# Average pooling on one core: runs of 126 KB per partition instead of 64 KB, and the stores moved into the load queue

## The chip, the cores and the metric

The kernel runs on one core of a Trainium2 chip. The metric is device time in microseconds (us) of one execution. The engines that matter are VectorE (DVE in the profile), which does the sums, ScalarE (ACT), which scales and issues some stores, SyncE (SP), which issues the loads, and the core's sixteen DMA engines, which move all data between HBM and the on-chip memory SBUF. A DMA that spans 128 partitions is spread over all sixteen DMA engines, eight partitions on each.

## The reference

Average pooling in one dimension with window 4 and stride 4 over float32 data of 64 x 256 x 8192:

```python
def reference(x, kernel_size, stride):          # 4 and 4
    out_len = (length - kernel_size) // stride + 1
    for i in range(out_len):
        start = i * stride
        output[:, :, i] = np.mean(x[:, :, start : start + kernel_size], axis=2)
```

The windows do not overlap and rows divide evenly, so the whole input can be taken as one flat run of 134,217,728 numbers, in which every four neighbours give one output. 536.87 MB are read and 134.22 MB written.

## The kernel before

The flat input is cut into 64 blocks. A block is 128 partitions of `RUN = 16384` numbers, 64 KB each and one behind the other in HBM, so it is 8 MB without a gap. Its output is 2 MB: 16 KB for each partition, again without a gap.

`load` issues one DMA of a whole block in SP's queue (line 44). Two input buffers `xt` are in turn. `sums` does two additions on VectorE: line 50 adds neighbours within `xt` and writes the half-size result over the front of the same tile; line 54 adds neighbours of that into an output tile `r`. `scale` (line 59) multiplies `r` by 1/4 in place on ScalarE. An output tile has room for two blocks, and there are two of them.

The order of the work is that of the program, engine by engine. SP issues a load when VectorE has finished line 54 for the block that was in that buffer. For the first `SINGLES = 8` blocks, ScalarE scales and stores each block by itself (line 75, 2 MB). After that it scales two blocks with one instruction and stores them with one DMA of 4 MB (line 78), in which each partition has two runs of 16 KB that lie 2 MB apart in HBM. All these stores are in ScalarE's own queue, so the DMA engines see two queues: SP's with loads and ScalarE's with stores.

At the end the last block is loaded in two pieces (`LAST`, 5 MB and 3 MB) into one buffer, and the last stores are issued by SP: a pair (line 87), a single block (line 90) and two pieces (line 95).

Of the kernel before, what the change touches and what calls it, by code (L numbers as in the profile page):

```python
# [1 line left out]

# [4 lines left out]


RUN = 16384

SINGLES = 8
LAST = (10240, 6144)


@with_exitstack
def kernel(
    ctx: ExitStack,
    tc: tile.TileContext,
    x: bass.AP,
    kernel_size: bass.AP,  # L20
    stride: bass.AP,
    out: bass.AP,
):
    nc = tc.nc
    K, S = int(kernel_size), int(stride)
    assert K == S == 4
    B, C, L = x.shape
    P = nc.NUM_PARTITIONS
    dt = x.dtype
    M = RUN // K  # L30
    blocks = B * C * L // (P * RUN)
    assert blocks * P * RUN == B * C * L and L % K == 0 and blocks % 2 == 0
    assert sum(LAST) == RUN

    xb = x.rearrange("b c l -> (b c l)").rearrange("(n p m) -> n p m", p=P, m=RUN)
    ob = out.rearrange("b c l -> (b c l)").rearrange("(n p m) -> n p m", p=P, m=M)

    pin = ctx.enter_context(tc.tile_pool(name="xin", bufs=2))
    pout = ctx.enter_context(tc.tile_pool(name="res", bufs=2))

    def load(i, a=0, b=RUN, xt=None):
        if xt is None:
            xt = pin.tile([P, RUN], dt, name="xt")
        nc.sync.dma_start(out=xt[:, a:b], in_=xb[i][:, a:b])
        return xt

    def sums(o, xt, a=0, b=RUN):
        v = xt[:, a:b].rearrange("p (m k) -> p m k", k=2)
        h = xt[:, a : (a + b) // 2]
        nc.vector.tensor_tensor(  # L50
            out=h, in0=v[:, :, 0], in1=v[:, :, 1], op=mybir.AluOpType.add
        )
        w = h.rearrange("p (m k) -> p m k", k=2)
        nc.vector.tensor_tensor(  # L54
            out=o, in0=w[:, :, 0], in1=w[:, :, 1], op=mybir.AluOpType.add
        )

    def scale(o):
        nc.scalar.mul(o, o, 1.0 / K)  # L59

    def edges(cuts):
        at = [sum(cuts[:j]) for j in range(len(cuts) + 1)]
        return list(zip(at[:-1], at[1:]))

    def both(i):
        return ob[i : i + 2].rearrange("n p m -> p n m")

    for i in range(0, blocks - 2, 2):
        r = pout.tile([P, 2, M], dt, name="r")
        for h in range(2):  # L70
            xt = load(i + h)
            sums(r[:, h, :], xt)
            if i < SINGLES:
                scale(r[:, h, :])
                nc.scalar.dma_start(out=ob[i + h], in_=r[:, h, :])
        if SINGLES <= i < blocks - 4:
            scale(r[:])
            nc.scalar.dma_start(out=both(i), in_=r[:])

    n = blocks - 1  # L80
    t = pout.tile([P, 2, M], dt, name="r")
    xt = load(n - 1)
    xl = None
    for a, b in edges(LAST):
        xl = load(n, a, b, xl)
    scale(r[:])
    nc.sync.dma_start(out=both(n - 3), in_=r[:])
    sums(t[:, 0, :], xt)
    scale(t[:, 0, :])
    nc.sync.dma_start(out=ob[n - 1], in_=t[:, 0, :])  # L90
    for a, b in edges(LAST):
        o = t[:, 1, a // K : b // K]
        sums(o, xl, a, b)
        scale(o)
        nc.sync.dma_start(out=ob[n][:, a // K : b // K], in_=o)


# [1 line left out]
_INS = ['x', 'kernel_size', 'stride']  # L99
_OUTS = [((64, 256, 2048), 'float32')]  # L100

_NUMBERS = {'kernel_size': 4, 'stride': 4}


# [26 lines left out]
```

## Time and profile before

| what | value |
|---|---|
| median of three runs | 1554.86 us (1554.7 to 1556.03) |
| the profiled execution, its own time | 1554.4 us |
| span of the profile | 1552.6 us |
| VectorE busy | 839.7 us (54%), 130 instructions |
| ScalarE busy | 227.4 us (15%), 39 instructions |
| data moved by DMA | 671.12 MB, mean 432 GB/s |
| a load of 8 MB, from issue to landing | 35.1 us (median) |
| a store of 4 MB by ScalarE, from issue to landing | 52.0 us (median) |
| line 50 on a block; line 54; line 59 on a block | 8.69 us; 4.43 us; 3.62 us |

The span runs from the first to the last event that the profile has of the core; the execution's time is 1.8 us longer. A DMA engine works off packets, each a contiguous piece of memory, and the profile counts them by queue: q1 is SP's, q10 is ScalarE's. "From issue to landing" includes the time in which a DMA stands in its queue behind others. An engine's waits are listed with what ended them, and SP's list is that of its DMA queue: a wait there delays the issue of a transfer, which matters only if the DMA engines have nothing else queued.

### The profile page before, as it was taken

Reading aid. Unit: us, or ns where it says so; the run is one execution under the profiler, and the core shown is the slowest. Engines: PE = TensorE matmul, PEld = TensorE weight load, DVE = VectorE, ACT = ScalarE, POOL = GpSimd, SP = SyncE. Lnnn points to the kernel's source line nnn. Section 1 sums busy time; section 2 is a strip of 40 time slices with the busy share of each in tenths; the row PEclk is TensorE's granted clock in tenths of the full one; section 3 lists DMA queues with packets and bytes.
Section 4 is the critical chain, followed back from the end, with each engine's and each line's share of the span. In section 5 each row is a group of like instructions: output and inputs, shape, how many; then the busy total and the mean of one; then the engine's idle time right before and its main releaser. Section 6 shows DMA issues by size and latency. Waiting matters only on the chain.

```text
span 1552.6 us, 471 instructions
## 1 busy us (share of the span) xinstructions
DVE 839.7 (54%) x130; ACT 227.4 (15%) x39; POOL 0.2 (0%) x4
## 2 busy tenths in 40 slices
DVE  3646556546465464654646546455464554645646
ACT  1111101110111101111011110111101111011111
POOL 0000000000000000000000000000000000000000
DMA  9999999999999999999999999999999999999999
GB/s 417 420 434 438 439 439 439 412 445 444 413 433 435 443 438 439 432 424 429 439 438 433 437 434 419 439 432 438 439 419 434 434 437 439 441 423 442 422 440 400
DMA packets 18292, 671.12 MB, mean 432 GB/s; under 512 B 1649, under 2 KB 1649, under 8 KB 1777
## 3 DMA queue, kind: packets, MB, share of 16 engines
q1 hardware_dynamic: 10064, 545.26, 81.1%
q10 hardware_dynamic: 8224, 125.83, 18.9%
q14 instruction: 4, 0.02, 0.0%
HBM read 536.87 MB, written 134.22 MB: 432 GB/s over the span
## 4 chain that ended last, share of the span: by engine, by line
DMA 71%; DVE 28%; issue 0%; ACT 0%; DVEq 0%
DMA xt<-in_x_dram 71%; DVE xt L50 18%; DVE r L54 9%; ACT r L59 0%; DVEq L54 0%
## 5 line engine op out<-in xcount | busy, mean ns | idle before, releaser
L50 DVE TENSOR_TENSOR xt<-xt 128x8192 f32<-128x8192 f32 (+1 forms) x65 | 556.5, 8561 | 696.1 <-DMA xt<-in_x_dram 696.1
L59 ACT ACTIVATE r<-r 128x8192 f32<-128x8192 f32 (+3 forms) x38 | 226.2, 5951 | 1313.0 <-DVE r L54 1313.0
L54 DVE TENSOR_TENSOR r<-xt 128x4096 f32<-128x4096 f32 (+1 forms) x65 | 283.4, 4360 | 3.9
L59 ACT ACT_TABLE_LOAD x1 | 1.3, 1283 | 0.7 <-PEq L112 0.7
L112 POOL MEMSET const-bfloat16-1.0<- 128x1 bf16 x1 | 0.1, 101 | 0.0
L112 POOL MEMSET const-uint8-127<- 128x1 uint8 x1 | 0.1, 101 | 0.0
L112 POOL MEMSET const-float32-0.0<- 128x1 f32 x1 | 0.1, 98 | 0.2 <-issue 0.2
L112 POOL MEMSET const-float32-1.0<- 128x1 f32 x1 | 0.1, 98 | 0.0
## 6 DMA issues: line engine op xcount, KB each, us to landing
out_dram<-r ACTq DMA_DIRECT2D x26, 4096.0 KB, 52.0
out_dram<-r ACTq DMA_DIRECT2D x8, 2048.0 KB, 31.7
xt<-in_x_dram SPq DMA_DIRECT2D x1, 5120.0 KB, 23.1
out_dram<-r SPq DMA_DIRECT2D x1, 4096.0 KB, 33.0
xt<-in_x_dram SPq DMA_DIRECT2D x1, 3072.0 KB, 30.0
out_dram<-r SPq DMA_DIRECT2D x1, 2048.0 KB, 16.9
out_dram<-r SPq DMA_DIRECT2D x1, 1280.0 KB, 12.9
xt<-in_x_dram SPq DMA_DIRECT2D x63, 35.1
```

The lines of the kernel that those rows point to most:

```text
L50: nc.vector.tensor_tensor(out=h, in0=v[:, :, 0], in1=v[:, :, 1], op=mybir.AluOpType.add)
L54: nc.vector.tensor_tensor(out=o, in0=w[:, :, 0], in1=w[:, :, 1], op=mybir.AluOpType.add)
L59: nc.scalar.mul(o, o, 1.0 / K)
L112: nc = _bacc.Bacc("TRN2", target_bir_lowering=False, num_devices=1)
```

## The change

- A unit of work is now a group: 128 partitions of 126 KB each, one behind the other in HBM. It is loaded in two halves, `h = 0` and `h = 1`, each 63 KB for every partition (`RUN = 16128`), so that the runs of one load lie 126 KB apart. The group's output is 31.5 KB for each partition, without a gap.
- There are 32 groups, and the rest of the data is one block of 64 KB for each partition (`END = 16384`), which is loaded in the two pieces that the last block had before.
- Every half is scaled by itself, right after its sums.
- The first four groups (`SINGLES = 4`) store each half by itself in ScalarE's queue, 15.75 KB for each partition.
- A later group is stored whole, with one DMA of 31.5 KB for each partition, in SP's queue: it is kept in `held` and issued behind the second load of the next group. The last group's store is issued behind the two loads of the end.

```diff
-RUN = 16384
+RUN = 16128
+END = 16384
 
-SINGLES = 8
+SINGLES = 4
...
-    xb = x.rearrange("b c l -> (b c l)").rearrange("(n p m) -> n p m", p=P, m=RUN)
-    ob = out.rearrange("b c l -> (b c l)").rearrange("(n p m) -> n p m", p=P, m=M)
+    xf = x.rearrange("b c l -> (b c l)")
+    of = out.rearrange("b c l -> (b c l)")
+    xb = xf[:body].rearrange("(n p h m) -> n p h m", p=P, h=2, m=RUN)
+    ob = of[: body // K].rearrange("(n p m) -> n p m", p=P, m=2 * M)
+    xe = xf[body:].rearrange("(p m) -> p m", p=P)
+    oe = of[body // K :].rearrange("(p m) -> p m", p=P)
...
-    for i in range(0, blocks - 2, 2):
-        r = pout.tile([P, 2, M], dt, name="r")
-        for h in range(2):
-            xt = load(i + h)
-            sums(r[:, h, :], xt)
-            if i < SINGLES:
-                scale(r[:, h, :])
-                nc.scalar.dma_start(out=ob[i + h], in_=r[:, h, :])
-        if SINGLES <= i < blocks - 4:
-            scale(r[:])
-            nc.scalar.dma_start(out=both(i), in_=r[:])
+    held = None
+    for g in range(groups):
+        r = pout.tile([P, 2 * M], dt, name="r")
+        for h in range(2):
+            xt = load(xb[g, :, h, :], 0, RUN)
+            if h == 1 and held is not None:
+                nc.sync.dma_start(out=ob[held[0]], in_=held[1])
+            o = r[:, h * M : (h + 1) * M]
+            sums(o, xt, 0, RUN)
+            scale(o)
+            if g < SINGLES:
+                nc.scalar.dma_start(out=ob[g][:, h * M : (h + 1) * M], in_=o)
+        if g >= SINGLES:
+            held = g, r[:]
...
-    scale(r[:])
-    nc.sync.dma_start(out=both(n - 3), in_=r[:])
-    sums(t[:, 0, :], xt)
-    scale(t[:, 0, :])
-    nc.sync.dma_start(out=ob[n - 1], in_=t[:, 0, :])
+    nc.sync.dma_start(out=ob[held[0]], in_=held[1])
+    e = pout.tile([P, 2 * M], dt, name="r")
     for a, b in edges(LAST):
-        o = t[:, 1, a // K : b // K]
+        o = e[:, a // K : b // K]
         sums(o, xl, a, b)
         scale(o)
-        nc.sync.dma_start(out=ob[n][:, a // K : b // K], in_=o)
+        nc.sync.dma_start(out=oe[:, a // K : b // K], in_=o)
```

More of the change, by code (lines that the diff above doesn't have):

```diff
@@ L30, with load, sums @@
     M = RUN // K
-    blocks = B * C * L // (P * RUN)
-    assert blocks * P * RUN == B * C * L and L % K == 0 and blocks % 2 == 0
-    assert sum(LAST) == RUN
-    xb = x.rearrange("b c l -> (b c l)").rearrange("(n p m) -> n p m", p=P, m=RUN)
-    ob = out.rearrange("b c l -> (b c l)").rearrange("(n p m) -> n p m", p=P, m=M)
+    total = B * C * L
+    groups = total // (2 * P * RUN)
+    body = groups * 2 * P * RUN
+    assert L % K == 0 and total - body == P * END
+    assert sum(LAST) == END
+    xf = x.rearrange("b c l -> (b c l)")
[4 more added lines that the diff above has]
+    oe = of[body // K :].rearrange("(p m) -> p m", p=P)
     pin = ctx.enter_context(tc.tile_pool(name="xin", bufs=2))
     pout = ctx.enter_context(tc.tile_pool(name="res", bufs=2))
-    def load(i, a=0, b=RUN, xt=None):
+    def load(src, a, b, xt=None):
         if xt is None:
-            xt = pin.tile([P, RUN], dt, name="xt")
-        nc.sync.dma_start(out=xt[:, a:b], in_=xb[i][:, a:b])
+            xt = pin.tile([P, END], dt, name="xt")
+        nc.sync.dma_start(out=xt[:, a:b], in_=src[:, a:b])
         return xt
-    def sums(o, xt, a=0, b=RUN):
+    def sums(o, xt, a, b):
         v = xt[:, a:b].rearrange("p (m k) -> p m k", k=2)
@@ L63, in edges @@
         return list(zip(at[:-1], at[1:]))
-    def both(i):
-        return ob[i : i + 2].rearrange("n p m -> p n m")
-    for i in range(0, blocks - 2, 2):
-        r = pout.tile([P, 2, M], dt, name="r")
+    held = None
+    for g in range(groups):
+        r = pout.tile([P, 2 * M], dt, name="r")
         for h in range(2):
-            xt = load(i + h)
-            sums(r[:, h, :], xt)
-            if i < SINGLES:
-                scale(r[:, h, :])
-                nc.scalar.dma_start(out=ob[i + h], in_=r[:, h, :])
-        if SINGLES <= i < blocks - 4:
-            scale(r[:])
-            nc.scalar.dma_start(out=both(i), in_=r[:])
-    n = blocks - 1
-    t = pout.tile([P, 2, M], dt, name="r")
-    xt = load(n - 1)
+            xt = load(xb[g, :, h, :], 0, RUN)
[8 more added lines that the diff above has]
+            held = g, r[:]
     xl = None
     for a, b in edges(LAST):
-        xl = load(n, a, b, xl)
-    scale(r[:])
-    nc.sync.dma_start(out=both(n - 3), in_=r[:])
-    sums(t[:, 0, :], xt)
-    scale(t[:, 0, :])
-    nc.sync.dma_start(out=ob[n - 1], in_=t[:, 0, :])
+        xl = load(xe, a, b, xl)
+    nc.sync.dma_start(out=ob[held[0]], in_=held[1])
+    e = pout.tile([P, 2 * M], dt, name="r")
     for a, b in edges(LAST):
-        o = t[:, 1, a // K : b // K]
+        o = e[:, a // K : b // K]
         sums(o, xl, a, b)
         scale(o)
-        nc.sync.dma_start(out=ob[n][:, a // K : b // K], in_=o)
+        nc.sync.dma_start(out=oe[:, a // K : b // K], in_=o)
 _INS = ['x', 'kernel_size', 'stride']
```

## The prediction

> **What bounds the kernel now.** I read the page first: its slices, its DMA queues and its chain. The last two columns of a queue's line are MB moved and the share of sixteen engines' span that its packets took.
>
> ```profile
> span 1552.6 us, 471 instructions
> DMA  9999999999999999999999999999999999999999
> DMA packets 18292, 671.12 MB, mean 432 GB/s; under 512 B 1649, under 2 KB 1649, under 8 KB 1777
> q1 hardware_dynamic: 10064, 545.26, 81.1%
> q10 hardware_dynamic: 8224, 125.83, 18.9%
> ```
>
> The DMA engines are full in every slice, and the two queues together take 100.0% of sixteen engines' span. VectorE is busy 54%, ScalarE 15%. (The chain of waits gives DMA 71% and VectorE 28%, but only because it steps from a load to the sums that freed its buffer; the queue was not empty meanwhile, as the waits below show.) The bytes are fixed (536.87 MB read, 134.22 MB written), so a change can act only through what the engines pay beside bytes: packets, gaps, start and end.
>
> The packet counts can be rebuilt. Queue 1 (SP) has 65 loads of 128 packets, one for each partition's whole run, which is 8320; its stores of the end have 256 + 128 + 128 + 128 = 640; and 69 DMAs leave 16 tiny ones each, 1104. The sum is 10064, as printed. Queue 10 (ScalarE) has 26 pair stores of 256, 8 single stores of 128 and 34 x 16: 8224. So a packet is one contiguous run of one partition: 64 KB in a load, 16 KB in a store.
>
> Then SP's waits (microseconds in total, times, longest):
>
> ```profile
> SPq L44 <- DVE r L54: 817.2, 62, 13.2
> SPq L44 <- DMA xt<-in_x_dram: 660.1, 62, 21.1
> ```
>
> SP issues a load when VectorE has freed its buffer, and a load takes 35.1 us from issue to landing (median of the page), against 19.3 us that one takes alone. So the next load is always queued before its turn, and these waits cost nothing.
>
> Last VectorE's timeline, for its first sum starts when a load has landed:
>
> ```profile
> 22.73 8.69 DVE L50 TENSOR_TENSOR xt<-xt 128x8192 f32<-128x8192 f32 x1 [22.73 <-DMA xt<-in_x_dram]
> 42.06 8.69 DVE L50 TENSOR_TENSOR xt<-xt 128x8192 f32<-128x8192 f32 x1 [6.18 <-DMA xt<-in_x_dram]
> ...
> 90.66 8.69 DVE L50 TENSOR_TENSOR xt<-xt 128x8192 f32<-128x8192 f32 x1 [11.07 <-DMA xt<-in_x_dram]
> ...
> 235.78 8.69 DVE L50 TENSOR_TENSOR xt<-xt 128x8192 f32<-128x8192 f32 x1 [10.97 <-DMA xt<-in_x_dram]
> 255.10 8.70 DVE L50 TENSOR_TENSOR xt<-xt 128x8192 f32<-128x8192 f32 x1 [6.17 <-DMA xt<-in_x_dram]
> ...
> 448.65 8.69 DVE L50 TENSOR_TENSOR xt<-xt 128x8192 f32<-128x8192 f32 x1 [11.07 <-DMA xt<-in_x_dram]
> ...
> 1513.12 8.69 DVE L50 TENSOR_TENSOR xt<-xt 128x8192 f32<-128x8192 f32 x1 [11.21 <-DMA xt<-in_x_dram]
> ```
>
> They give three prices. A load with no store beside it takes 42.06 - 22.73 = 19.33 and 255.10 - 235.78 = 19.32 us. A load and a single 2 MB store take (235.78 - 90.66) / 6 = 24.187, so the store costs 4.862. Two loads and a 4 MB pair store take (1513.12 - 448.65) / 22 = 48.385, so that store costs 9.735.
>
> **Rate and packet price.** Twice the single store (9.724) is the pair store (9.735), though it is two DMAs and not one: the price goes by packets and bytes, not by DMAs. A load (8.389 MB) and a single store (2.097 MB) both have 8 packets on each engine, so their difference is bytes alone: 6.291 MB in 14.463 us, 435.0 GB/s. What is left of the single store, 4.862 - 2.097/0.4350 = 0.041 us, is 8 packets at 5.1 ns. The same 0.041 fits the load.
>
> **The change, part by part.** *Runs of 63 KB and stores of 31.5 KB.* Data packets on each engine before: 520 of loads and 64 + 432 + 24 = 520 of stores, 1040 in all. After: loads 64 x 8 + 16 = 528, stores 8 x 8 + 28 x 8 + 16 = 304, together 832. That is 208 fewer; at 5.1 ns, 1.06 us saved. DMAs go from 103 to 104, which by the step above is nothing. Packets of 63 and 31.5 KB lie between sizes that are in the trace.
>
> *The pitch.* A group is now 126 KB for each partition, so neighbouring partitions are no longer 64 KB apart. No row has this pitch. It cannot gain more than all that the packets cost beside bytes, 1040 x 5.1 ns = 5.3 us. For a loss the nearest bound is the slowest block of the settled part, 24.6 against 24.2 us (1102.51 from 1077.91), which on every block would be 64 x 0.4 = 26 us. I take 0, because loads 64 KB apart and stores 16 KB apart fit one rate.
>
> *Stores in SP's queue.* The order becomes load h0, load h1, store of the group before. One load is 8.258 MB / 435.0 + 0.041 = 19.02 us, a store 9.53, a group 47.58. Count from the landing of h0. The load of h1 lands at 19.02, the old store at 28.55, the next h0 at 47.58. VectorE takes 8.69 + 4.43 us, less 1.6%: 12.9. So the next h0 is issued at 12.9 and has its turn at 28.55; the next h1 is issued at 31.9, turn 47.58: 15.6 us early each. The store waits for ScalarE's second half (3.6 us), is issued at 35.6 and has its turn at 66.6. Behind this new wait in SP's stream stands the next h0 load, which has to wait for VectorE until 60.5 anyway. The buffer of r is free when the old store lands at 28.55, and VectorE writes it next at 56. Nothing here runs the queue dry.
>
> What no row shows is a load behind a store in one queue. Below, the cost is 0: packets of both kinds alternate now, from two queues, and the pair store's 16 packets cost 9.735 - 4.194/0.4350 = 0.094 us in all. At the tail of before, the other hand-over is in one queue: issue plus landing puts the 3072 KB load at 1532.3 and the 4096 KB store behind it at 1542.0, 9.7 us, which is the undisturbed price. Above, it is a whole restart: the first load of all took 22.0 us from issue to landing, 2.67 more than 19.33. I take 0, by the nearer rows, and keep 28 x 2.67 = 75 us as the far end.
>
> *The start.* Four groups still go out as single halves by ScalarE: 8 stores as before, 1.6% smaller; 0.
>
> *ScalarE and VectorE.* Scaling by halves is 27 times two instructions of 3.62 us for one of 7.03, and one more block is two more sums. ScalarE stood idle 1313 us waiting for VectorE, VectorE 696 us waiting for loads: 0. Without that cover it would be 27 x 0.2 = 6 us.
>
> *The end.* Let T be the landing of the last whole half. The queue holds store 9.5, pieces 12.1 and 7.3, store 9.5: busy to T + 38.4. The first piece lands at T + 21.6; its sums (5.48 + 2.83) and scaling (2.34) let its store go at T + 32.3. The second piece's sums start at T + 29.9, take 3.35 + 1.77, then 1.48: its store goes at T + 36.5, needed at T + 41.5. The queue stays full: 0. The slack of the last store is 5 us, where it was 8.7 before (issued 1541.2, its forerunner landed 1549.9).
>
> **Sum.** -1.06 us and five zeros. The profiled execution took 1554.4 us, of which 1552.6 are span; its forecast is 1551.5 of span and 1553.3 in all. The median, 1554.86, is 0.5 above that execution; less 1.1 it is 1553.8. A measurement of this kernel can tell about 0.2%, 3.1 us, from no change, so the forecast is no change.
>
> **Rivals.** *A, slower: the loads behind a store start late.* In one queue, each of 28 hand-overs from writing HBM to reading it leaves the engines idle. For it: the row does not exist, and 2.67 us is what a start costs. Against it: the alternating packets, and at the tail a store behind a store (4096 then 2048 KB, landings 1542.0 and 1546.9) takes 4.9 us, with no room for a pause. It decides from (3.1 + 1.1) / 28 = 0.15 us each; a fifth of a restart, 0.53 us, gives 1553.8 + 15 = 1569; a whole one 1629. Chance 0.20. The Trainium skill speaks for this rival (DMA: Bandwidth & Descriptors, "Anatomy of one DMA"): a semaphore fires only when the last byte is confirmed, most of a fixed 2 us, longest towards HBM; if the confirmation held the loads behind, an estimate by that page is 28 x 2 = 56 us, while the tail's 4.9 us says that nothing behind is held.
>
> *B, faster: what I call packet price is a price of the pitch.* Then runs 126 KB apart lose it all, 5.3 us: 1549.6. For it: VectorE's starts swing between 23.6 and 24.6 us from block to block, so something beside packets moves. Against it: loads and stores with pitches of 64 and 16 KB fit one line. Chance 0.18. The Trainium skill has a rule for this (same page, "Latency and other measured facts"): row pitches of 512 KiB and more at powers of two slow DMA down, and a few KiB of padding restores it; 64 KiB is below its list, and the 19.33 us are 434 GB/s.
>
> *C, slower: the last store or SP's new wait comes late.* It decides when more than the 5 us at the end, or 15 us in a group, are lost; the end would cost up to 5 us more, 1559. Nothing in the trace takes that long. Chance 0.04.
>
> **How the numbers follow.** No change 0.58, faster 0.18 (B), slower 0.24 (A and C). The range starts at B's 1549.5 and goes up to 1562, 0.3 us at each hand-over, leaving out the dearer half of A.
>
> **What would show it.** Right: 832 x 16 data packets and 104 x 16 tiny ones, 14,980 packets with the four of instructions; queue 10 near 2.5%; loads landing in turns of 19.0 and 28.6 us, 47.6 a group; a store about 40 us from issue to landing; a span near 1551.5. Wrong: the long turn above 28.7 us (A), the short one below 18.98 (B), or a slice below 9 at the end (C).

## The result, and the profile after

The changed kernel takes 1558.0 us (median of 19 runs, 1557.04 to 1559.54), the kernel before 1554.64 (19 runs, 1554.23 to 1556.27). The ratio is 1.0020, with a 95% interval of 1.0014 to 1.0026: 3.4 us slower, where no change was forecast, and 4.2 us above the 1553.8 to which the prediction's sum came.

The page of the changed kernel has the counts that were forecast, but for one packet:

```profile
span 1556.8 us, 480 instructions
DMA  9999999999999999999999999999999999999998
DMA packets 14979, 671.12 MB, mean 431 GB/s; under 512 B 1664, under 2 KB 1664, under 8 KB 1792
q1 hardware_dynamic: 13824, 654.58, 97.3%
q10 hardware_dynamic: 1152, 16.52, 2.5%
```

There are 3313 packets fewer (a load's run is 63 KB; the 126 KB of the title are what a group takes of one partition), and ScalarE's queue is down to 2.5% of the DMA time. But the last slice shows 8 where it was 9, and the two queues add up to 99.8% of a longer span: the engines are no longer all full to the end.

SP's waits (microseconds in total, times, longest) have the new one:

```profile
SPq L51 <- DVE r L61: 817.8, 63, 13.0
SPq L51 <- DMA xt<-in_x_dram: 566.4, 63, 21.1
SPq L78 <- ACT r L66: 87.7, 27, 3.3
```

It is 3.3 us a group, where 3.6 was worked out, and delays no load: loads take 34.6 us from issue to landing and stores 40.6 (medians of the page), against 34.7 and 40.5 by the prediction's sums. The landings themselves, in VectorE's timeline:

```profile
41.73 8.56 DVE L57 TENSOR_TENSOR xt<-xt 128x8064 f32<-128x8064 f32 x1 [6.10 <-DMA xt<-in_x_dram]
67.39 8.56 DVE L57 TENSOR_TENSOR xt<-xt 128x8064 f32<-128x8064 f32 x1 [12.71 <-DMA xt<-in_x_dram]
...
1207.85 8.56 DVE L57 TENSOR_TENSOR xt<-xt 128x8064 f32<-128x8064 f32 x1 [15.60 <-DMA xt<-in_x_dram]
1226.89 8.56 DVE L57 TENSOR_TENSOR xt<-xt 128x8064 f32<-128x8064 f32 x1 [6.03 <-DMA xt<-in_x_dram]
1255.45 8.56 DVE L57 TENSOR_TENSOR xt<-xt 128x8064 f32<-128x8064 f32 x1 [15.61 <-DMA xt<-in_x_dram]
...
1493.66 8.56 DVE L57 TENSOR_TENSOR xt<-xt 128x8064 f32<-128x8064 f32 x1 [15.61 <-DMA xt<-in_x_dram]
```

The turns shown are 19.04 and 28.56 us, forecast 19.02 and 28.55; late in the run a group takes (1493.66 - 1207.85) / 6 = 47.64, forecast 47.58. Two things are off. The third block lands 25.66 us after the second, where a load and a single store should take 23.81: 1.85 us lost in one block. And from 301.07 us (the first h0 after the first store in SP's queue) to 1493.66, 25 groups take 47.70 each, 0.12 more than forecast, most of it before 1200 us. Of these 3.1 us, 2.5 lie in the short turns, from h0 to h1, which hold nothing but a load and end where a store sets in. The longest short turn is 19.40 us, and the long turn behind it is 28.63:

```profile
348.72 8.56 DVE L57 TENSOR_TENSOR xt<-xt 128x8064 f32<-128x8064 f32 x1 [15.66 <-DMA xt<-in_x_dram]
368.12 8.56 DVE L57 TENSOR_TENSOR xt<-xt 128x8064 f32<-128x8064 f32 x1 [6.39 <-DMA xt<-in_x_dram]
396.75 8.56 DVE L57 TENSOR_TENSOR xt<-xt 128x8064 f32<-128x8064 f32 x1 [15.67 <-DMA xt<-in_x_dram]
```

**Which engines are late.** A landing is that of the last of sixteen DMA engines. Each leaves a tiny packet under 512 B when its share of a DMA is done, so counting those in a window shows how far apart the engines are. This is the last whole half of the changed kernel, first from 1506.5 to 1508.2 us, then from 1508.2 to 1512.4:

```profile
DMA packets 28, 0.61 MB, mean 361 GB/s; under 512 B 12, under 2 KB 12, under 8 KB 12
...
DMA packets 60, 1.87 MB, mean 445 GB/s; under 512 B 4, under 2 KB 4, under 8 KB 4
```

And the last whole block of the kernel before, where a store ends at the same time, in the windows from 1511.3 to 1512.3 and from 1512.3 to 1512.7 (two DMAs, so 32 marks):

```profile
DMA packets 45, 0.61 MB, mean 615 GB/s; under 512 B 30, under 2 KB 30, under 8 KB 30
...
DMA packets 3, 0.04 MB, mean 102 GB/s; under 512 B 2, under 2 KB 2, under 8 KB 2
```

Twelve engines of the changed kernel are done in the first window, the other four only in the 4.2 us behind it. Read from the marks one by one, the last engine is 5.35 us behind the first and 4.79 behind the median; before, 1.02 and 0.84. Below, "spread" is the distance from the first engine to the last at a load, and "lag" the last engine's distance from the median one, at the last whole load where no other is named. The bytes of every engine are the same and the last engine has work to the end, so the engine that has lost most sets the end.

The end shows it. The rows have 40 slices of 0.19 us, for the kernel before from 1545 to 1552.6 us and for the changed kernel from 1549.2 to 1556.8; a packet counts whole in the slice in which it starts. A single packet of the last store in a slice is too little for a digit above 0, but stands in the second row as 32 GB/s:

```profile
DMA  9479989999999999998898999999722000000000
```

```profile
DMA  2521299998999792212020200000000000000000
GB/s 108 224 108 54 108 442 377 410 377 377 507 410 410 313 442 97 86 65 86 0 86 32 86 32 32 32 32 32 0 32 32 32 32 0 0 0 0 0 0 0
```

Before, the engines finish within about 1 us of each other. After, twelve are done by 1552.3 us, and one is still at its packets until 1555.7. The low slices at the front have another cause. The last store was issued only at 1549.35 us, for it hangs on the last load, which lands when the last engine is done, and by then most engines had finished all that was queued: the first five slices, up to 1550.1 us, show how little was left. That pause costs nothing, for the last engine was still at the stores before.

**The account.** An undisturbed packet's time in the trace goes by its size (a 65536 B one 2418 ns, a 16384 B one 611 ns, a 32256 B one 1194 ns), and delayed ones stand out; below, a packet is late when it took over 20 ns more than is usual for its size. Summed over the run and divided by sixteen, the delays come to 1.0 us before and 2.2 after, 1.2 more for an average engine. The lag is 3.95 more. The fewer packets save 1.06 by the prediction's price. Together that is 4.1 us; the spans differ by 4.2. The sum closes better than it deserves: counted from the average engine, as the 1.2 us are, the last one is 3.5 us further behind than before (4.21 against 0.74), which makes 3.6. In the same way e2 below comes to 3.9 of 4.1 us and e6 to 1.7 of 1.8, but e8 to 3.6 where its span is only 2.3 longer. So the account shows where the time went, not every part of it.

**Where packets are delayed.** After the start, from 300 to 1510 us, 70 packets of the changed kernel are late. 56 of them lie within 3 us of the point where the first engine is done with a load and a store sets in behind it in SP's queue, in windows that hold 16% of the packets; 52 of the 56 are packets of loads, on engines that are still loading while others have begun to store. Of the other 14, 13 lie as near to the point where the loads set in again.

### The profile page after: what moved, and what is told of

It reads as the page before. It is cut to its first block, busy times and chain, and to the rows that moved or that the text cites. A ratio compares the mean times of both kernels' runs of the same rounds, so it can differ in the third digit from the quotient of the medians.

```text
span 1556.8 us, 480 instructions
## 1 busy us (share of the span) xinstructions
DVE 840.0 (54%) x132; ACT 233.1 (15%) x67; POOL 0.2 (0%) x4
## 4 chain that ended last, share of the span: by engine, by line
DMA 72%; DVE 27%; issue 0%; ACT 0%; DVEq 0%
DMA xt<-in_x_dram 72%; DVE xt L57 18%; DVE r L61 9%; ACT r L66 0%; DVEq L61 0%
## 5 line engine op out<-in xcount | busy, mean ns | idle before, releaser
L57 DVE TENSOR_TENSOR xt<-xt 128x8064 f32<-128x8064 f32 (+1 forms) x66 | 556.6, 8433 | 703.7 <-DMA xt<-in_x_dram 703.7
L66 ACT ACTIVATE r<-r 128x4032 f32<-128x4032 f32 (+1 forms) x66 | 231.8, 3512 | 1315.5 <-DVE r L61 1315.5
L61 DVE TENSOR_TENSOR r<-xt 128x4032 f32<-128x4032 f32 (+1 forms) x66 | 283.5, 4296 | 4.0
## 6 DMA issues: line engine op xcount, KB each, us to landing
xt<-in_x_dram SPq DMA_DIRECT2D x64, 8064.0 KB, 34.6
out_dram<-r SPq DMA_DIRECT2D x28, 4032.0 KB, 40.6
```

The lines of the kernel that those rows point to most:

```text
L57: nc.vector.tensor_tensor(out=h, in0=v[:, :, 0], in1=v[:, :, 1], op=mybir.AluOpType.add)
L61: nc.vector.tensor_tensor(out=o, in0=w[:, :, 0], in1=w[:, :, 1], op=mybir.AluOpType.add)
```

## The experiments

The ratios are to the kernel before, with their 95% intervals. Three theories were tested first: Q, the hand-overs in SP's queue; P, the pitch of 126 KB; S, the start. Then, as results came in, what larger store runs do in ScalarE's queue.

**e1_scalar_queue:** the new layout, stores back in ScalarE's queue.

```diff
-        if g >= SINGLES:
+        if SINGLES <= g < groups - 1:
+            nc.scalar.dma_start(out=ob[g], in_=r[:])
+        elif g == groups - 1:
             held = g, r[:]
```

> The changed kernel's layout (126 KB groups, 31.5 KB store runs), with the stores of groups 4 to 30 issued by ScalarE's queue after the second scaling; only the last group's store stays in SP's queue. Theory Q (the hand-over from loads to stores within one queue lets single DMA engines fall behind, 5.35 us by the end): the lag stops growing when the start is over, so 2.6 us or more come back, and the time is 1553.5 to 1555.5. Theory P (the pitch of 126 KB makes engines collide, whatever the queue): as slow as the changed kernel, 1557 to 1558.5. Theory S (the lag comes from the start, where it is already 2.4 us at the seventh load): 1557.

Measured: 1570.92 us, 1.011 (1.0096 to 1.0125). All three theories missed it: this is 13 us slower than the changed kernel. Over 700 packets are late after 300 us, 16 us for an average engine. The new layout needs SP's queue; something else in it is bad for ScalarE's.

**e2_old_layout_sp:** the old layout, stores moved to SP's queue.

```diff
+    held = None
     for i in range(0, blocks - 2, 2):
...
             xt = load(i + h)
+            if h == 1 and held is not None:
+                nc.sync.dma_start(out=both(held[0]), in_=held[1])
...
         if SINGLES <= i < blocks - 4:
             scale(r[:])
-            nc.scalar.dma_start(out=both(i), in_=r[:])
+            held = i, r[:]
```

> The kernel before with its 64 KB blocks, 16 KB store runs and scaling of pairs, but the pair stores issued by SP, each behind the second load of the next pair. Theory Q: slower than before by 3 to 5 us, 1557.5 to 1559.5, with a spread of several us between the first and the last engine's completion of a load. Theory P: as before, 1554.6. Theory S: as before, 1554.6.

Measured: 1558.52 us, 1.0024 (1.0014 to 1.0033), as theory Q had it: the queue alone costs 4.0 us, with runs, pitch and packets as before. Its page:

```profile
span 1556.7 us, 446 instructions
q1 hardware_dynamic: 17136, 654.32, 97.4%
q10 hardware_dynamic: 1152, 16.78, 2.5%
```

The engines end the seventh load 0.39 us apart, as in the kernel before, and the last whole one 4.24 apart (lag 3.3); 103 of 113 late packets from 300 to 1510 us lie within 3 us of a store's setting in. The first store in SP's queue, at 273.6 us, sets in without a late packet; at the second there are fifteen, from 319.5 us on. The edit changes two things that belong together: the queue, and that a store now starts only when both loads of the next pair are through.

**e3_no_singles:** no stores by ScalarE at all.

```diff
-SINGLES = 4
+SINGLES = 0
```

> The changed kernel with SINGLES = 0: no store goes by ScalarE, the first group's store too is issued by SP behind the second load of the next group. Theory S: the lag of the start is gone, 1555.5 to 1556. Theory Q: four more hand-overs and nothing else, 1558 to 1559. Theory P: 1558.

Measured: 1557.41 us, 1.0019 (1.0011 to 1.0028), lag 3.1. Nearer to the changed kernel than to what theory S gave. The third block now lands 19.05 us after the second, without loss, but the fourth lands 20.12 us after the third, where 19.02 is the price: 1.1 us are lost when the first store sets in. So a loss at the first store, if a smaller one, does not need ScalarE's queue.

**e4_half_stores_sp:** twice as many hand-overs.

```diff
-            if h == 1 and held is not None:
-                nc.sync.dma_start(out=ob[held[0]], in_=held[1])
+            if held is not None:
+                nc.sync.dma_start(
+                    out=ob[held[0]][:, h * M : (h + 1) * M],
+                    in_=held[1][:, h * M : (h + 1) * M],
+                )
```

> The changed kernel with each later group's store split into its two halves (15.75 KB runs), one behind each load in SP's queue, so that there are twice as many hand-overs between loads and stores, of half the size. Packets: 28 x 8 more on each engine at 5 ns, 1.1 us more. Theory Q: the lag grows twice as fast, 1561 to 1563. Theory P and S: the packets alone, 1559.

Measured: 1557.61 us, 1.0019 (1.001 to 1.0028). Theory Q's size was wrong: doubling the hand-overs costs nothing more. The 1559 of theories P and S is missed too, so the 1.1 us for more packets do not show either. The spread reaches 3.80 us by 417 us and then stays at 3.80 until the last whole load. So the lag is not a price that each hand-over pays; it builds up and then stops growing. That the engines by then stand in an order in which hand-overs no longer delay them is a guess that no run tests.

**e5_pitch128_scalar:** e1 with powers of two, 128 KB groups and 32 KB store runs.

```diff
 # against e1_scalar_queue
-RUN = 16128
+RUN = 16384
...
-    groups = total // (2 * P * RUN)
+    groups = total // (2 * P * RUN) - 1
...
```

> As e1_scalar_queue, but with RUN = 16384: groups of 128 KB per partition, stores of 32 KB runs by ScalarE's queue; the last two blocks are stored as in the kernel before. Theory B (engines stall where stores set in or stop; they stay in step only while every load packet has a store packet behind it; a 32 KB run halves the packets of a store, so it is used up after one load and the second load runs alone): as slow as e1, 1567 to 1573. Theory L (the pitch of 126 KB is to blame with two queues): like the kernel before, 1554 to 1556. Theory R (a store run of about 32 KB between load packets is to blame by its size): 1567 to 1573.

Measured: 1568.54 us, 1.0102 (1.0067 to 1.0137): not the 126 KB.

**e6_all_singles** and **e7_two_halves_scalar:** the new loads, with 15.75 KB store runs in ScalarE's queue.

```diff
 # e6, against the changed kernel
-SINGLES = 4
+SINGLES = 31
 # e7, against e1_scalar_queue
-            nc.scalar.dma_start(out=ob[g], in_=r[:])
+            for j in (0, M):
+                nc.scalar.dma_start(out=ob[g][:, j : j + M], in_=r[:, j : j + M])
```

> The changed kernel with SINGLES = 31: all groups but the last are stored by halves of 15.75 KB runs in ScalarE's queue, 8 packets behind each load of 8 packets. Theory B: no stalls after the start, 1554.5 to 1556. Theory L: 1567 to 1573. Theory R: 1554.5 to 1556.

> As e1_scalar_queue (126 KB groups, stores in ScalarE's queue after the second scaling), but each group is stored by two DMAs of 15.75 KB runs, one right behind the other: 16 packets for two loads again, without a break. Theory B: 1554.5 to 1556. Theory L: 1567 to 1573. Theory R: 1554.5 to 1556.

Measured: 1556.14 us, 1.0008 (0.9998 to 1.0018), and 1556.09, 1.0007 (0.9998 to 1.0016). Each interval just includes no change; the medians are 1.6 us above the kernel before. Theory L falls: beyond the start, loads 126 KB apart are harmless with short store runs. Both keep the loss of the start (spread 2.3 and 2.5 us at the seventh load) and it hardly changes from there.

**e8_pitch63_pairs:** runs of 63 KB, 63 KB apart.

```diff
 # against e1_scalar_queue
-    xb = xf[:body].rearrange("(n p h m) -> n p h m", p=P, h=2, m=RUN)
-    ob = of[: body // K].rearrange("(n p m) -> n p m", p=P, m=2 * M)
+    xb = xf[:body].rearrange("(n h p m) -> n p h m", p=P, h=2, m=RUN)
+    ob = of[: body // K].rearrange("(n h p m) -> n p h m", p=P, h=2, m=M)
...
```

> As e7_two_halves_scalar, but the halves of a group are two blocks as in the kernel before, with runs 63 KB apart in the loads and 15.75 KB apart in the stores, stored in pairs by one DMA of ScalarE's queue. All theories: 1554 to 1556. It tells whether the lag of the start (2.4 us at the seventh load with runs 126 KB apart, 0.4 us with 64 KB) comes from the pitch: then it is near 0.4 here, otherwise 2.

Measured: 1556.68 us, 1.0009 (1.0 to 1.0019), slightly above the range that all theories gave. The engines end the seventh load 2.2 us apart, so the loss of the start does not come from 126 against 64 KB. It comes with 63 KB, by its size or by where its runs begin. After 300 us only three packets are late, each 0.3 us behind a packet that fetches instructions, and yet the spread ends at 3.6 to 4.2 us; what of the 1556.68 is theirs stays open.

**e11_63_of_64:** 63 KB runs that begin at multiples of 64 KB.

```diff
+PART = 16128
+Q = PART // 4
...
-    def load(i, a=0, b=RUN, xt=None):
+    def load(i, a=0, b=PART, xt=None):
...
-            nc.scalar.dma_start(out=both(i), in_=r[:])
+            nc.scalar.dma_start(out=both(i)[:, :, :Q], in_=r[:, :, :Q])
...
```

> The kernel before, but only 63 KB of every 64 KB run is loaded and 15.75 KB of every 16 KB stored (the last window sums of each run are left out; the two last pieces are loaded whole). Addresses start at multiples of 64 KB, the size is that of the changed kernel. If the size makes the lag of the start, the sixteen engines end the seventh load 2 us apart and the third block lands 25.5 us after the second; if it is the start addresses, 0.4 us apart and 24.0 us after. Time near 1531 either way.

Measured: 1530.86 us. VectorE's timeline of e7 and of e11, second and third block:

```profile
41.82 8.56 DVE L57 TENSOR_TENSOR xt<-xt 128x8064 f32<-128x8064 f32 x1 [6.10 <-DMA xt<-in_x_dram]
67.35 8.56 DVE L57 TENSOR_TENSOR xt<-xt 128x8064 f32<-128x8064 f32 x1 [12.58 <-DMA xt<-in_x_dram]
```

```profile
41.43 8.56 DVE L52 TENSOR_TENSOR xt<-xt 128x8064 f32<-128x8064 f32 x1 [6.10 <-DMA xt<-in_x_dram]
65.54 8.56 DVE L52 TENSOR_TENSOR xt<-xt 128x8064 f32<-128x8064 f32 x1 [11.16 <-DMA xt<-in_x_dram]
```

25.53 us with runs that begin anywhere, 24.11 with runs of the same size that begin at multiples of 64 KB; the spread at the seventh load is 0.34. So the size is not the cause. The third block loses 1.4 us more in e7, and 1.6 in the changed kernel, where the runs are off the multiples of 64 KB (those of the loads, or those of the stores off the multiples of 16 KB: both moved).

**e9_half_the_outputs** and **e13_half_stored_126:** pauses in the stores, without long runs.

```diff
 # e9, against the kernel before
-            nc.scalar.dma_start(out=both(i), in_=r[:])
+            nc.scalar.dma_start(out=ob[i], in_=r[:, 0, :])
 # e13, against e1_scalar_queue
-            nc.scalar.dma_start(out=ob[g], in_=r[:])
+            nc.scalar.dma_start(out=ob[g][:, :M], in_=r[:, :M])
```

> The kernel before, but from block 8 on only the first block of each pair is stored (26 stores of 2 MB instead of 26 of 4 MB; the other half of those outputs is left out). Runs stay at 16 KB, so a store is used up after one load, and the second load of a pair runs alone. Without stalls: 1554.5 - 26 x 4.862 = 1428.1. Theory B (setting in and stopping of stores): many stalls after an instruction packet has pushed one engine back, as in e5: 1433 to 1442. Theory R (the run of 32 KB): no stalls, 1427 to 1430.

> As e7_two_halves_scalar, but of groups 4 to 30 only the first half is stored (27 stores of 15.75 KB runs; the other halves of those outputs are left out), so that the second load of a group runs alone, with loads 126 KB apart. Without stalls: 1556.1 - 27 x 4.786 = 1426.9. Theory R (only a store run of about 32 KB in ScalarE's queue stalls the engines): 1426 to 1428. Theory BP (a wide pitch together with stores that set in and stop): 1435 to 1442.

Measured: 1428.93 us and 1427.2 us. Theory B and theory BP fall: stores that set in and stop cost nothing by themselves, at either pitch. Both sums (1428.1 and 1426.9) hold to 0.8 and 0.3 us.

**e14_32k_runs_old_loads:** long store runs and nothing else.

```diff
     def both(i):
-        return ob[i : i + 2].rearrange("n p m -> p n m")
+        return ob[i : i + 2].rearrange("n p m -> (n p m)").rearrange("(p m) -> p m", p=P)
...
```

> The kernel before with one change: the 4 MB of a pair are stored as one run of 32 KB per partition instead of two of 16 KB (the outputs of a pair land in another order, the bytes are the same). Loads, queues and times of issue stay. Theory R: 1565 to 1573, as e5. Theory BP: 1553.5 to 1555, the loads being 64 KB apart.

Measured: 1565.58 us, 1.0070 (1.0055 to 1.0085). Theory R stands. From its page and its timeline:

```profile
out_dram<-r ACTq DMA_DIRECT2D x26, 4096.0 KB, 33.1
```

```profile
1111.75 8.69 DVE L50 TENSOR_TENSOR xt<-xt 128x8192 f32<-128x8192 f32 x1 [15.26 <-DMA xt<-in_x_dram]
1160.82 8.69 DVE L50 TENSOR_TENSOR xt<-xt 128x8192 f32<-128x8192 f32 x1 [15.33 <-DMA xt<-in_x_dram]
...
1501.60 8.69 DVE L50 TENSOR_TENSOR xt<-xt 128x8192 f32<-128x8192 f32 x1 [15.02 <-DMA xt<-in_x_dram]
```

The store lands after 33.1 us and not 52.0, which fits turns between one load packet and one store packet of twice the bytes: 8 x (2.42 + 1.2) = 29 us of packets for a store, in place of 16 x (2.42 + 0.61) = 48 (an estimate from the times of packets above). A pair takes (1501.60 - 1111.75) / 8 = 48.73 us and not 48.385.

**e10_pitch128_sp:** the changed kernel with runs that begin at multiples of 64 KB.

```diff
 # against e5_pitch128_scalar
-        if SINGLES <= g < groups - 1:
-            nc.scalar.dma_start(out=ob[g], in_=r[:])
-        elif g == groups - 1:
+        if g >= SINGLES:
             held = g, r[:]
```

> The changed kernel with RUN = 16384 (128 KB groups, 32 KB store runs, stores in SP's queue as in the changed kernel), and the end of the kernel before. If 63 KB runs cost 1.6 to 1.9 us at the start and SP's hand-overs the rest, this takes 1556 to 1556.5. If the start costs nothing by itself, 1558.

Measured: 1557.31 us, 1.0017 (1.0008 to 1.0026), between the two. Its interval reaches over both forecasts, so it does not decide between them. The start is clean (spread 0.54 at the seventh load). Afterwards the lag grows by 2.4 us to 2.8, about as in the changed kernel (by 2.6, to 4.8), but the late packets after 300 us come to 2.1 us for an average engine, where they are 0.7 there. So a clean start does not leave the rest as it was.

**e12_more_instructions:** e5 with four times the scalings.

```diff
-        nc.scalar.mul(o, o, 1.0 / K)
+        w = o.shape[1] // 4
+        for j in range(4):
+            p = o[:, j * w : (j + 1) * w]
+            nc.scalar.mul(p, p, 1.0 / K)
```

> e5_pitch128_scalar with each scaling in four pieces on ScalarE, which adds some 200 instructions to an engine that is idle otherwise. If the packets that fetch instructions push one engine back and the breaks in the stores make it worse from there (in e5 nothing happened before 559 us, the first such packet), the first packet comes earlier, the stalls begin with it, and the time is 1570 to 1576. If the stalls come by themselves after some 600 us: 1568.5 as e5.

Measured: 1568.89 us (1567.81 to 1578.21), no clear difference from e5's 1568.54. The first instruction packet came at 258 us, and the first packet over 200 ns late at 366, against 559 in e5. In e14 it came at 305, before any instruction packet. So such a packet is not needed for the stalls, and whether it hastens them stays open.

No version that writes all outputs in their places beat the kernel before; the nearest are e6 and e7, 1.6 us above it.

## Why the prediction was wrong, point by point

**Rate: right; packet price: untested.** 435.0 GB/s and 5.1 ns a packet gave the undisturbed turns of the changed kernel to 0.02 us, and the prices of loads and stores gave the two kernels with half the stores to 0.8 us or better.

**Fewer packets, -1.06 us: not shown.** It is one of the three terms of the account, but no run shows it by itself: e4 has 216 more packets on each engine than the changed kernel and is 0.4 us faster.

**"The pitch ... I take 0": the failed step of the start.** The distance alone, of which that step and rival B spoke, does not decide: runs 63 KB apart (e8) lose as those 126 KB apart do, and runs 128 KB apart (e10) start clean. Nor does the size (e11). What is left is whether the runs begin at multiples of 64 KB, or whether their distance is such a multiple; the two go together in all runs here and were not told apart. Off the multiples, the first stores push engines apart: 1.85 us are lost in the third block here, 0.3 in e11. e6 and e7 have this loss and none of the hand-overs, and their medians are 1.6 us above the kernel before. Rival B had the sign the wrong way round. The Trainium skill's rule for pitches at large powers of two (DMA: Bandwidth & Descriptors, "Latency and other measured facts"), named beside it, begins at 512 KiB and advises leaving such pitches by a few KiB. It says nothing of 64 KB, where the runs here go the other way: 0.3 to 0.5 us of spread on the multiples and 2.2 to 2.5 off them.

**"What no row shows is a load behind a store in one queue ... I take 0": the failed step of the settled part.** The cost is there, 0.12 us a group, just under the 0.15 that rival A needed by itself. But rival A had it at the wrong hand-over. Its sign, a long turn above 28.7 us, shows in one of 25. The time is lost at the other hand-over, from load to store (56 of 70 late packets, and 2.5 of 3.1 us in the turns that end there), which the prediction took as priced by one undisturbed case at the tail. e2 shows that moving the stores into SP's queue suffices, 4.0 us. Nor is it a restart that is paid each time: e4 doubled it for nothing. It is delay of single engines that adds up on the slowest. Rival A's estimate of 56 us rested on 2 us of the Trainium skill (DMA: Bandwidth & Descriptors, "Anatomy of one DMA"), which that section gives for DMAs issued by GpSimd, not by SP or ScalarE. The runs here show nothing of that size: 0.12 us a group.

**The step that was not there.** The sum treated sixteen engines as one. Their mean was full, so a delay of one engine had no row. The lag is 4.79 us in place of 0.84, and that difference is larger than the result, 3.4. That 1558.0 lies inside the stated range is in part luck: the range's upper end stands for 0.3 us at each hand-over, and some of the loss comes from the start, for which the sum had nothing.

**New waits, ScalarE, VectorE: right. The end: right for the last engine alone.** The waits are 3.3 us a group and hide. The last store went out 36.7 us after the landing of the last whole half, forecast 36.5, and the last engine had 5 us of work left, as forecast. But the sum had the queue full to the end for all engines, and twelve of them paused before the last store. The last slice below 9, which was to be the sign of rival C, showed, though not by C's cause: no late store lengthened the run, the lag of the last engine did.

**What stays open.** The queue and the runs off the multiples of 64 KB each cost something alone (4.0 us, and 1.6 by the medians, against the kernel before), and together hardly more than the queue (3.4, or 4.5 if the fewer packets save what was forecast). Why an engine that still loads is held up while others store, and why the order of the engines settles, no run tells. The larger store runs, counted as a gain, cost 11 us in ScalarE's queue (e14); in SP's queue no run shows a gain by them, and e4, with half the run, is no slower than the changed kernel.

## What to carry to other kernels

In a kernel that is bound by DMA, look beside the mean at the completion marks of one transfer: how far the sixteen engines are apart at its landing, and whether that grows, tells what no share of busy time shows. Bytes and packet counts price a DMA well, but the order in which loads and stores meet on an engine (which queue, how long a run, whether on multiples of 64 KB) moved this kernel by 1.6 to 16 us at equal bytes. Change one of these at a time, since two that are harmless or cheap alone can be dear together, and the other way round.

## What the runs showed of the hardware that was not expected

A store run of 32 KB in a second queue beside 64 KB loads is slower than two of 16 KB: 1565.58 against 1554.46 us. In the kernel before, the three packets over 200 ns late after 300 us (at 560.0, 695.9 and 914.1 us, by 0.53, 0.25 and 0.30 us) come 0.3 us after the start of the three packets of 8 KB in that part that the profile counts as instructions. The first is in the window from 559.5 to 560.5 us of the DMA queues (a packet counts whole where it starts, so a share can exceed 100%):

```profile
q1 hardware_dynamic: 16, 1.05, 245.1%
q14 instruction: 1, 0.01, 1.9%
```

At the first of them the spread of the engines rose from 0.43 to 1.02 us, and it did not fall below 1.0 again up to the last whole load.
